# Softmax minus one-hot on one core: 512 columns of the sixth row load on ACT's queue, and ACT's first six rows are written out ahead of its loop

## The chip, the cores and the metric

The kernel runs on one core of one Trainium2 chip. The metric is the device time of one execution in microseconds (us), the median over several runs; smaller is better. The core has five engines with instruction streams of their own: PE (TensorE), DVE (VectorE), ACT (ScalarE), POOL (GpSimd) and SP (SyncE). Transfers between the chip's memory and the core's on-chip memory run on 16 DMA engines. SP and ACT each have a queue on which they issue such transfers.

## The reference

The kernel computes the gradient of the cross entropy: for each of 8 x 1024 rows of 8192 logits, the softmax, less 1 at the row's label.

```
logits_max = np.max(logits, axis=-1, keepdims=True)
exp_logits = np.exp(logits - logits_max)
softmax = exp_logits / np.sum(exp_logits, axis=-1, keepdims=True)
...
one_hot[batch_idx, seq_idx, labels] = 1.0
return (softmax - one_hot).astype(np.float32)
```

Input and output are fp32, 268.4 MB each. Each number is read once and written once.

## The kernel before

**Tiling.** The 8192 rows of the problem are cut into 64 tiles of 128 rows, one row for each of the 128 partitions. The code counts these tiles with t, and the text calls one of them "a row": 128 x 8192 fp32, 4 MB, 32 KB in each partition. Two neighbouring tiles (j = 0 and 1) interleave in memory. The on-chip buffer X holds six rows: SLOTS = 3 times G = 2, so R = 6, and row t lives in slot k = t % 6.

**Steps of a row.** All are done in place in the slot:

1. load (lines 114 to 119): SP issues it on its queue. From row 6 on it waits until the store of the slot's previous row has landed (semaphore `put`). Row 5 waits for `w_iota` instead: an iota of 8192 int16 numbers is first made in the first half of slot 5 and copied from there into PSUM by DVE.
2. `row_max` (line 121): DVE, negated maximum over the row, waits for the load (semaphore `got`).
3. `row_exp` (line 127): ACT, exponential with the maximum as bias, with the row sum accumulated.
4. `invert` (line 133): DVE, reciprocal of the sum.
5. `row_scale` (line 139): ACT, multiplies the row by it.
6. `subtract` (line 145): DVE, subtracts 1 where the iota equals the label.
7. `store` (line 152): ACT issues it on its own queue, after waiting for the subtraction (semaphore `sub`).

**Order.** It is written out by hand; semaphores connect the engines. SP issues all 64 loads in the order of the rows, one behind the other. DVE and ACT each do row 0's maximum and exponential ahead, and then run a hardware loop of ROUNDS = 10 rounds with six rows in each, sixty rows in all. In DVE's loop (lines 172 to 180) row k's turn is: `invert` of row k, `row_max` of row k + 1, `subtract` of row k. In ACT's loop (lines 183 to 192) it is: `row_scale` of row k, `row_exp` of row k + 1, `store` of row k. The counts that the semaphores have to reach are held in registers (`done`, `landed`) that each round raises. The last four rows stand behind the loops; the very last one is scaled and subtracted in four quarters and stored in two halves.

Every operation goes through the helper `run` (line 56), which gives all waits but the last to the engine as instructions of their own and the last one to the operation. That is why nearly every row of the profile carries line 67.

Of the kernel before, what the change touches and what calls it, by code (L numbers as in the profile page):

```python
# [8 lines left out]
G = 2  # L9
SLOTS = 3  # L10
R = SLOTS * G


LAST = 4


@with_exitstack
def kernel(
# [6 lines left out]
    nc = tc.nc  # L25
# [8 lines left out]
    N, V = x_nv.shape  # L34
# [3 lines left out]
    x_b = x_nv.rearrange("(b p j) v -> b p j v", p=P, j=G)  # L38
    o_b = o_nv.rearrange("(b p j) v -> b p j v", p=P, j=G)
# [16 lines left out]
    with tc.tile_critical():  # L56
        sem = tc.alloc_semaphore
        got = [[sem(f"got{i}{q}") for q in range(2)] for i in range(SLOTS)]
        put = [[sem(f"put{i}{q}") for q in range(2)] for i in range(SLOTS)]
        lab_got, dve, pe, pool = (sem(n) for n in ("lab_got", "dve", "pe", "pool"))  # L60
        count = {}

        def run(engine, waits, counter, method, **operands):

            for w in waits[:-1]:
                engine.wait_ge(*w)
            instruction = getattr(engine, method)(**operands)  # L67
            for w in waits[-1:]:
                instruction._wait_ge(*w)
            step = 16 if method == "dma_start" else 1  # L70
            instruction.then_inc(counter, step)
            count[counter.name] = count.get(counter.name, 0) + step
            return counter, count[counter.name]
# [6 lines left out]
            out=ident[:], in_=ident[:], compare_op=Alu.not_equal, fill=1.0,  # L80
# [10 lines left out]
        for j in range(G):  # L91
            w = run(
                nc.tensor, [w_ident, w_lab], pe, "transpose",
                out=lab_ps[:, j, :], in_=lab_f[:, j, :], identity=ident[:],
# [4 lines left out]
            out=iota[:].bitcast(i32), in0=made.bitcast(i32), scalar1=0, scalar2=None, op0=Alu.bitwise_or,  # L99
# [6 lines left out]
        max_of, exp_of, inv_of, scl_of, sub_of = map(per_parity, ("max", "exp", "inv", "scl", "sub"))  # L106

        def slot(k):
            return X[:, k // G, k % G, :]

        def column(a, k):
            return a[:, k : k + 1]

        def load(t):
            b, j = divmod(t, G)
            k = t % R
            after = [(put[k // G][q], t // R * 16) for q in range(G)] if t >= R else []
            after = after[j : j + 1] or [w_iota] * (t == R - 1)
            run(nc.sync, after, got[k // G][j], "dma_start", out=slot(k), in_=x_b[b, :, j, :])

        def row_max(k, n):
            run(
                nc.vector, [(got[k // G][k % G], n)], max_of[k % G], "tensor_reduce",
                out=column(m, k), in_=slot(k), axis=mybir.AxisListType.X, op=Alu.max, negate=True,
            )

        def row_exp(k, n):
            run(
                nc.scalar, [(max_of[k % G], n)], exp_of[k % G], "activation", out=slot(k),
                in_=slot(k), func=Act.Exp, bias=column(m, k), scale=1.0, accum_out=column(s, k),  # L130
            )
# [7 lines left out]
        def row_scale(k, n, c=slice(0, V)):  # L139
            run(  # L140
                nc.scalar, [(inv_of[k % G], n)], scl_of[k % G], "activation", out=slot(k)[:, c],
                in_=slot(k)[:, c], func=Act.Copy, bias=0.0, scale=column(r, k),
            )
# [8 lines left out]
        def store(k, n, target, c=slice(0, V)):  # L152
            run(
                nc.scalar, [(sub_of[k % G], n)], put[k // G][k % G], "dma_start",
                out=target[:, c], in_=slot(k)[:, c],
            )

        def counter(engine, first):
            reg = engine.alloc_register(f"from{first}")
            engine.reg_mov(reg, first)  # L160
            return reg

        ROUNDS = T // R
        for t in range(T):
            load(t)

        row_max(0, 16)
        row_exp(0, 1)

        done = [counter(nc.vector, q + 1) for q in range(SLOTS)]  # L170
        landed = counter(nc.vector, 16)
        with nc.vector.Fori(0, ROUNDS * SLOTS, SLOTS) as b:  # L172
            for k in range(R):
                invert(k, done[k // G])
                if k == R - 1:
                    nc.vector.reg_add(landed, landed, 16)
                row_max((k + 1) % R, landed)
                subtract(k, done[k // G], lab[:, k % G, bass.ds(b + k // G, 1)])
            for reg in done:
                nc.vector.reg_add(reg, reg, SLOTS)  # L180

        done = [counter(nc.scalar, q + 1) for q in range(SLOTS)]
        with nc.scalar.Fori(0, ROUNDS * SLOTS, SLOTS) as b:
            for k in range(R):
                row_scale(k, done[k // G])
                if k == R - 1:
                    for reg in done[: SLOTS - 1]:
                        nc.scalar.reg_add(reg, reg, SLOTS)
                row_exp((k + 1) % R, done[(k + 1) % R // G])
                target = o_b[bass.ds(b + k // G, 1), :, k % G, :]  # L190
                store(k, done[k // G], target.rearrange("o p v -> (o p) v"))
            nc.scalar.reg_add(done[-1], done[-1], SLOTS)

        for t in range(ROUNDS * R, T - 1):
            k, n = t % R, t // G + 1
            invert(k, n)
            row_max(k + 1, 16 * (ROUNDS + 1))
            row_scale(k, n)
            row_exp(k + 1, n + k % G)
            subtract(k, n, lab[:, t % G, t // G : t // G + 1])  # L200
            store(k, n, o_b[t // G, :, t % G, :])
        k, n = (T - 1) % R, B
        invert(k, n)
        for q in range(4):
            c = slice(q * V // 4, (q + 1) * V // 4)
# [41 lines left out]
```

## Time and profile before

| what | value |
|---|---|
| median of three runs | 1247.6 us (1247.5 to 1247.87) |
| span of the profiled execution | 1245.6 us |
| DVE busy in it | 1121.8 us (90%) |
| ACT busy in it | 919.4 us (74%) |
| bytes moved | 268.50 MB read, 268.44 MB written |

The span counts from the first to the last instruction of one profiled execution. It is 2.0 us below the median of the runs, and the steps of that execution are compared with its own span.

How to read the rows: a row of the timeline has the start in us, the duration, the engine, the line, the operation, and its output and input as "out<-in" with partitions x elements; the square brackets give idle time of the engine ahead of it, and what ended that. A "q" behind an engine's name (ACTq, SPq, DVEq) means its sequencer, which issues transfers, does register work and waits. A row of stretches has the stretch, its length, then for PE, its weight loads, DVE, ACT and POOL the busy time with a count of instructions, then PE's clock, the DMA engines' share of busy time and GB/s. A row of a DMA queue has packets, MB and the share of 16 engines' time; q1 is SP's queue, q10 ACT's. A packet is counted where it ends, so in short stretches the share can be over 100%.

### The profile page before, as it was taken

How to read it: one execution, taken by the hardware profiler on the slowest of the kernel's cores; microseconds unless marked ns; L12 is line 12 of the kernel's file. 1: busy time of each engine (PE TensorE's matmuls, PEld its weight loads, DVE VectorE, ACT ScalarE, POOL GpSimd, SP SyncE). 2: the span in 40 equal slices, each digit the busy share in tenths (PEclk: the TensorE clock that was granted, in tenths of full speed). 3: DMA queues.
4: the chain of work that ended last, by engine and by line, in shares of the span. 5: the costliest groups of instructions: out<-in, count | busy, mean ns of one | idle time of the engine just before them, and what ended most of it. 6: DMA issues, size and time to landing. Idle time of an engine off the chain costs nothing.

```text
span 1245.6 us, 868 instructions
## 1 busy us (share of the span) xinstructions
PE 0.4 (0%) x2; PEld 0.3 (0%) x2; DVE 1121.8 (90%) x198; ACT 919.4 (74%) x196; POOL 7.4 (1%) x7
## 2 busy tenths in 40 slices
PE   0000000000000000000000000000000000000000
PEld 0000000000000000000000000000000000000000
DVE  5999999999988989889898898988988989889893
ACT  3888888888767777777767777677777777777772
POOL 2000000000000000000000000000000000000000
DMA  9999999999999999999999999999999999999999
GB/s 406 418 426 436 438 434 425 438 438 429 429 438 436 427 434 438 435 426 436 438 432 426 438 438 428 430 438 435 428 434 438 434 427 436 437 434 426 438 436 389
DMA packets 18625, 536.95 MB, mean 431 GB/s; under 512 B 2080, under 2 KB 2080, under 8 KB 2112
## 3 DMA queue, kind: packets, MB, share of 16 engines
q1 hardware_dynamic: 9216, 268.44, 50.0%
q10 hardware_dynamic: 9408, 268.51, 49.9%
q14 instruction: 1, 0.01, 0.0%
HBM read 268.50 MB, written 268.44 MB: 431 GB/s over the span
## 4 chain that ended last, share of the span: by engine, by line
another core or an unknown queue 67%; DVE 21%; DMA 6%; issue 2%; SPq 1%; DVEq 0%; ACT 0%; ACTq 0%; PE 0%
DVE m L67 11%; DVE X L67 10%; DMA out_dram<-X 4%; DMA X<-in_logits_dram 2%; SPq L67 1%; DVE iota L67 0%; DVE lab_f L67 0%; DMA lab_raw<-in_labels_dram 0%; DVEq L56 0%; ACT X L67 0%; DVE r L67 0%; PE iota L67 0%; ACTq L67 0%; DVEq L172 0%
## 5 line engine op out<-in xcount | busy, mean ns | idle before, releaser
L67 DVE TENSOR_REDUCE m<-X 128x1 f32<-128x8192 f32 x64 | 555.6, 8681 | 90.6 <-DMA X<-in_logits_dram 90.6
L67 ACT ACTIVATE X<-X,m 128x8192 f32<-128x8192 f32 x64 | 455.8, 7122 | 184.8 <-DVE m L67 184.8
L67 DVE SCALAR_TENSOR_TENSOR X<-iota,lab,X 128x8192 f32<-128x8192 int16 (+1 forms) x67 | 559.8, 8360 | 2.4 <-ACT X L67 2.4
L67 ACT ACTIVATE X<-X,r 128x8192 f32<-128x8192 f32 (+1 forms) x67 | 456.4, 6816 | 118.2 <-DVE r L67 118.2
L67 DVE RECIPROCAL r<-s 128x1 f32<-128x1 f32 x64 | 9.8, 153 | 7.3 <-ACT X L67 7.3
L67 ACT ACTIVATION_READ_ACCUMULATOR X<-X,m 128x1 f32 x64 | 11.9, 186 | 0.0
L67 DVE CAST lab_f<-lab_raw 32x256 f32<-32x256 int32 x1 | 3.8, 3784 | 4.6 <-DMA lab_raw<-in_labels_dram 4.6
L67 POOL IOTA X<- 128x8192 int16 x1 | 6.9, 6943 | 0.0
L67 DVE TENSOR_SCALAR iota<-X 128x4096 int32<-128x4096 int32 x1 | 4.4, 4428 | 0.1
L67 ACT ACT_TABLE_LOAD x1 | 1.3, 1283 | 1.4 <-SPq L56 1.4
L67 DVE COPY lab<-iota 128x64 f32<-128x64 f32 x1 | 0.2, 225 | 0.5 <-PE iota L67 0.5
L67 PE MATMUL iota<-ident,lab_f 32*128 32x32 f32 x2 | 0.4, 298 | 8.5 <-DVE lab_f L67 8.5
L67 PEld LDWEIGHTS iota<-ident,lab_f 32*128 32x128 f32 x2 | 0.3, 192 | 8.4 <-DVE lab_f L67 8.4
L67 POOL TENSOR_SCALAR_AFFINE_SELECT ident<-ident 32x32 f32<-32x32 f32 x1 | 0.2, 202 | 0.1
L67 POOL MEMSET ident<- 32x32 f32 x1 | 0.1, 114 | 0.5 <-SPq L56 0.5
L231 POOL MEMSET const-bfloat16-1.0<- 128x1 bf16 x1 | 0.1, 107 | 0.0
L231 POOL MEMSET const-uint8-127<- 128x1 uint8 x1 | 0.1, 107 | 0.0
L231 POOL MEMSET const-float32-0.0<- 128x1 f32 x1 | 0.1, 104 | 0.2 <-issue 0.2
L231 POOL MEMSET const-float32-1.0<- 128x1 f32 x1 | 0.1, 104 | 0.0
## 6 DMA issues: line engine op xcount, KB each, us to landing
X<-in_logits_dram SPq DMA_DIRECT2D x64, 4096.0 KB, 24.2
out_dram<-X ACTq DMA_DIRECT2D x63, 4096.0 KB, 55.2
out_dram<-X ACTq DMA_DIRECT2D x2, 2048.0 KB, 16.9
lab_raw<-in_labels_dram ACTq DMA_DIRECT2D x1, 64.0 KB, 3.7
```

The source lines that it names most:

```text
L67: instruction = getattr(engine, method)(**operands)
L231: nc = _bacc.Bacc("TRN2", target_bir_lowering=False, num_devices=1)
```

## The change

Three things change.

The load of row 5 is split. SP loads the first 7680 of its 8192 columns, at the same place in its queue and behind the same wait. The other 512 columns (`SLAB`; 128 pieces of 2 KB, 256 KB in all) are loaded by a new function `load_rest`, issued on ACT's queue with a semaphore of its own, `rest_got`, and no wait.

`row_max` of slot 5 waits for `rest_got` to reach 16 ahead of its wait for `got`. The instruction stands in DVE's loop, so it is met in each of the ten rounds, though `rest_got` is raised only once.

ACT's first six rows are written out ahead of its loop, with constants as semaphore counts and addresses; `load_rest` stands among them, after the exponential of row 1 and ahead of the store of row 0. The loop runs over the remaining nine rounds, and its counters begin at SLOTS + 1 and up. DVE's loop keeps its ten rounds. A constant `LAST`, which nothing used, is gone.

```
-LAST = 4
+SLAB = 512
...
-        lab_got, dve, pe, pool = (sem(n) for n in ("lab_got", "dve", "pe", "pool"))
+        lab_got, dve, pe, pool, rest_got = (sem(n) for n in ("lab_got", "dve", "pe", "pool", "rest_got"))
...
-            run(nc.sync, after, got[k // G][j], "dma_start", out=slot(k), in_=x_b[b, :, j, :])
+            c = slice(0, V - SLAB) if t == R - 1 else slice(0, V)
+            run(nc.sync, after, got[k // G][j], "dma_start", out=slot(k)[:, c], in_=x_b[b, :, j, c])
+
+        def load_rest():
+            c = slice(V - SLAB, V)
+            run(
+                nc.scalar, [], rest_got, "dma_start",
+                out=slot(R - 1)[:, c], in_=x_b[SLOTS - 1, :, G - 1, c],
+            )
 
         def row_max(k, n):
+            rest = [(rest_got, 16)] if k == R - 1 else []
             run(
-                nc.vector, [(got[k // G][k % G], n)], max_of[k % G], "tensor_reduce",
+                nc.vector, rest + [(got[k // G][k % G], n)], max_of[k % G], "tensor_reduce",
                 out=column(m, k), in_=slot(k), axis=mybir.AxisListType.X, op=Alu.max, negate=True,
             )
...
-        done = [counter(nc.scalar, q + 1) for q in range(SLOTS)]
-        with nc.scalar.Fori(0, ROUNDS * SLOTS, SLOTS) as b:
+        for t in range(R):
+            k, n = t % R, t // G + 1
+            row_scale(k, n)
+            row_exp((k + 1) % R, (t + 1) // G + 1)
+            if t == 0:
+                load_rest()
+            store(k, n, o_b[t // G, :, t % G, :])
+
+        done = [counter(nc.scalar, SLOTS + q + 1) for q in range(SLOTS)]
+        with nc.scalar.Fori(SLOTS, ROUNDS * SLOTS, SLOTS) as b:
             for k in range(R):
                 row_scale(k, done[k // G])
                 if k == R - 1:
```

## The prediction

> **What bounds the kernel now.** I read the page first: span, DMA row, bytes, chain.
>
> ```profile
> span 1245.6 us, 868 instructions
> ...
> PE 0.4 (0%) x2; PEld 0.3 (0%) x2; DVE 1121.8 (90%) x198; ACT 919.4 (74%) x196; POOL 7.4 (1%) x7
> ...
> DMA  9999999999999999999999999999999999999999
> ...
> HBM read 268.50 MB, written 268.44 MB: 431 GB/s over the span
> ...
> another core or an unknown queue 67%; DVE 21%; DMA 6%; issue 2%; SPq 1%; DVEq 0%; ACT 0%; ACTq 0%; PE 0%
> ```
>
> The DMA engines are busy in all forty slices; no compute engine is. The chain's largest share carries no name, so the chain in order of time comes next, with the longest wait of SP's own queue:
>
> ```profile
> 254.75 8.58 DVE m L67
> ...
> 272.02 49.67 DMA out_dram<-X
> 321.71 0.33 SPq L67
> 322.04 18.97 another core or an unknown queue
> 341.02 0.33 SPq L67
> ...
> 1174.07 24.22 DMA X<-in_logits_dram
> 1198.31 8.69 DVE m L67
> ```
> ```profile
> SPq L67 <- DMA out_dram<-X: 1140.4, 58, 57.2
> ```
>
> From 322 us on the piece without a name lies between one load's issue and the next, and SP's queue says what it waits for: a store that has to land, 58 times. Up to 272 the chain runs through DVE. That could suggest that the early part is bound by DVE, so I asked for the rate by stretch (the last two numbers are DMA share and GB/s):
>
> ```profile
> 3.00:47.00 44.00, 0.41 (x2) 0.28 (x2) 34.49 (x9) 21.55 (x5) 5.25 (x1) 1.00 1.00 429
> 47.00:71.00 24.00, 0.00 (x0) 0.00 (x0) 24.00 (x5) 20.66 (x4) 0.00 (x0) 1.00 1.00 415
> 71.00:272.00 201.00, 0.00 (x0) 0.00 (x0) 201.00 (x37) 165.71 (x36) 0.00 (x0) 1.00 1.00 433
> 322.00:1174.00 852.00, 0.00 (x0) 0.00 (x0) 765.87 (x133) 630.46 (x133) 0.00 (x0) 1.00 1.00 433
> 1198.00:1233.00 35.00, 0.00 (x0) 0.00 (x0) 26.54 (x7) 20.74 (x7) 0.00 (x0) 1.00 1.01 435
> ```
>
> The engines are as full where DVE leads the chain (433 GB/s) as where the loads wait for stores (433). So the whole time is bytes over rate. DVE is only the first to be asked in a stretch where six preloaded slots give it work. A change counts if it changes the bytes, what a packet costs, or leaves both DMA queues empty at once.
>
> How the queues share the engines: in steady work, the 20 us from 342, and in three successive microseconds from 57 to 60:
>
> ```profile
> q10 hardware_dynamic: 144, 4.19, 48.6%
> q1 hardware_dynamic: 144, 4.19, 48.6%
> ```
> ```profile
> q1 hardware_dynamic: 16, 0.52, 121.3%
> q10 hardware_dynamic: 16, 0.52, 121.3%
> q1 hardware_dynamic: 16, 0.52, 121.3%
> ```
>
> q1 is SP's queue (loads), q10 ACT's (stores). A row is 144 packets: 128 of 32 KB and 16 tiny ones, so 8 + 1 for each engine. The queues take turns packet by packet: sixteen of one, then sixteen of the other. 121.3% of 16 engines for 1 us over 16 packets is 1.21 us a packet, and 16 x 1.21 = 19.4 us is the distance between loads in the chain (322.04 to 341.02 with the issue, 19.3).
>
> **The change part by part.** The span ends with the stores' last bytes, so I sum against 1245.6.
>
> *Bytes.* The slab, 128 rows of 2 KB, leaves SP's sixth load and goes to ACT's queue: none saved, none added. An engine's eight packets of row 5 shrink from 32 to 30 KB: by the rate 8 x 1.21 / 16 = 0.61 us less. It gets eight packets of 2 KB more. Before has such packets, the labels' 32, in the first 5 us:
>
> ```profile
> q10 hardware_dynamic: 48, 0.07, 5.0%
> ...
> lab_raw<-in_labels_dram ACTq DMA_DIRECT2D x1, 64.0 KB, 3.7
> ```
>
> 5.0% of 16 x 5 us is 4.0 us of engine time over 32 packets (the 16 tiny ones are next to nothing): 0.125 us each. Eight are 1.00 us. Net +0.4 us. From below: packets at the bulk rate, 0.076 us each, net 0. From above: the slab holds every engine as long as the label load took from issue to landing, 3.7 - 0.6 = +3.1. I take +0.4, since the label packets are of the same size.
>
> *When the slab starts, and what stands behind it.* It has no wait of its own, but stands behind the second exponential on ACT:
>
> ```profile
> 38.32 7.12 ACT L67 ACTIVATE X<-X,m 128x8192 f32<-128x8192 f32 x1 [1.46 <-DVE m L67]
> 46.97 0.39 ACTq L67 DMA_DIRECT2D out_dram<-X  x1
> ...
> 98.86 8.67 DVE L67 TENSOR_REDUCE m<-X 128x1 f32<-128x8192 f32 x1
> ...
> 116.17 8.67 DVE L67 TENSOR_REDUCE m<-X 128x1 f32<-128x8192 f32 x1
> ```
> ```profile
> L67 ACTq MOVE out_dram<-X x60: 29/29/35, 38.4 to 1149.0; - x60
> ```
>
> ACT's sequencer computed the first store's address at 38.4, while the exponential had only begun; so the slab issues near 38.4 and costs the sequencer about the 0.39 us of a store's issue, in time in which it waits for DVE until 46.97. SP's queue is full then, so eight small packets take turns with eight of 32 KB: 8 x (1.21 + 0.13) = 10.7 us, after a start of 2.5 (worked out below), landing near 52. Row 5's maximum starts at 98.86, so DVE's new wait finds the slab landed with some 46 us in hand; all that DVE does is queued behind that wait, which is why this margin matters. The first store is asked for at 46.97 and can wait behind the slab's last packets for about 2 us (47 + 2.5 against 52). Late next is then the load of row 6, which SP issues when that store has landed (71.22), and behind it in SP's queue every later load:
>
> ```profile
> 71.22 18.47 SPq L67 DMA_DIRECT2D X<-in_logits_dram  x2
> ```
>
> It lands some 24 us later, near 95, for a maximum at 116.17: 20 us in hand. SP moves exactly the bytes that ACT's queue did not, so the engines stay full. Cost 0.
>
> *First bytes.* There is a dip where the first store joins:
>
> ```profile
> 48.00:52.00 4.00, 0.00 (x0) 0.00 (x0) 4.00 (x1) 4.00 (x1) 0.00 (x0) 1.00 0.89 279
> 52.00:56.00 4.00, 0.00 (x0) 0.00 (x0) 4.00 (x2) 2.90 (x2) 0.00 (x0) 1.00 1.03 442
> ```
>
> (433 - 279) x 4 us is 0.62 MB, or 1.4 us; a window cuts packets of 0.52 MB, so this is rough (1.0 us by the row from 47 to 71). With the slab, ACT's queue joins earlier and lightly: between -1.4 (the dip goes) and +1.4 (it comes twice). I take 0, as the store joins all the same.
>
> *Fixed start of a DMA.* The first two loads:
>
> ```profile
> DMA to landing us min/median/max: 12.2/16.9/21.5
> ```
>
> 12.2 us for eight packets of 1.21 leaves 2.5 us of start and finish. The second, queued behind it, took 21.5, only 9.3 more, so that latency overlaps and takes no engine time. The Trainium skill ("DMA: Bandwidth & Descriptors", section "Anatomy of one DMA") gives each DMA a fixed cost of about 2.0 us, which speaks against splitting one. If all of it fell on the engines, the sum would be 2.0 us above before, an estimate from that page; the row shows it as latency under other work, and I don't add it.
>
> *ACT's loop, DVE's wait.* Six rows written out drop six rounds of address arithmetic on ACT; DVE gets a second wait before row 5's maximum, once in each of ten rounds, about as dear as its existing register step:
>
> ```profile
> L67 DVEq FUSED_REGOPS  x60: 53/57/71, 29.6 to 1140.2; - x60
> ...
> DVE m L67 <- DMA X<-in_logits_dram: 90.6, 47, 2.0
> ```
>
> At 0.07 us, two or three fall in DVE's stretch before 272 (0.2 us, hidden by the queued stores), the others in the up to 2.0 us that DVE then waits for each load. Without that cover, 0.7 us in all. Cost 0.
>
> *The end.* Would a delay of the computation reach it? The last row's two half stores are issued from 1222.74; packets of SP and ACT in 1226 to 1232, then 1232 to 1238:
>
> ```profile
> q10 hardware_dynamic: 80, 2.62, 101.1%
> ```
> ```profile
> q10 hardware_dynamic: 155, 2.54, 98.7%
> ```
>
> 80 packets of 32 KB are still whole rows; only then come the 16 KB packets of the half rows. So the last row stands in the queue for some 10 us, less 2.5 of start: 7 us of delay are free.
>
> Sum: 1245.6 + 0.4 = 1246.0. The runs' median, 1247.6, is 2.0 above the span, so **1248.0**; its own range, with the dip's -1.4 and the slab's +3.1, is 1246.2 to 1250.7.
>
> **The rivals.**
>
> *A. The slab doesn't go early.* ACT could issue it only after the exponential, at 45.5. Its eight turns would last until 57 and the first store would stand behind them, 6 us late; load 6 too, against 20 us in hand. The loads meanwhile have the engines alone (429 in the row of 3 to 47). Again 1248.0. For it: the slab stands behind that instruction. Against: the address step at 38.4. By the Trainium skill (same page, "Queues, rings and completion order") an engine drains a packet of 9 to 17 descriptors before it switches queues; the slab, nine for each engine, would then be through in a microsecond and A could not happen. The rows from 57 to 60 show turns of one 32 KB piece, so the trace does not agree.
>
> *B. Slower: the engines lose step.* A row's semaphore is complete when the slowest of 16 engines is. If unequal packets (2 and 30 KB) leave engines apart, each hand-over from store to load comes late, and the 415 GB/s of 47 to 71 hold on to 272, where the chain leaves DVE: 201 x (433/415 - 1) = 8.7 us, so 1248.0 + 8.7 = 1256.7. It decides from the point at which the rate after 71 drops below 433 by 1.2%. For it: 279 GB/s where the queues met. Against: 442 right after.
>
> *C. Faster: a better pitch.* Loads alone, from 3.8 to 48 us:
>
> ```profile
> DMA packets 670, 19.33 MB, mean 437 GB/s; under 512 B 80, under 2 KB 80, under 8 KB 80
> ```
>
> If the shift of one sixteenth of a row let the mixture run at 437 from 71 to 1198: 1127 x (1 - 433/437) = 10.3 us less, 1237.7. For it: some rate is left. Against: turns are by packet whatever the shift, and stores alone reach 435 at most.
>
> **How the numbers follow.** 0.2%, or 2.5 us, is about what a measurement of this kernel tells from no change: 1245.1 to 1250.1. Forecast 0.66, A 0.12, B 0.14, C 0.08. Forecast and A end within the bound: same 0.78, slower 0.14, faster 0.08. The 80% range reaches a little to both sides, for partial B or C: 1244.5 to 1251.5.
>
> **What would show it.** Right: a load of 256 KB issued near 38.4 and landing near 52; DVE's maximum of row 5 at about 98.9 without idle time; 19.4 us from load to load; 433 GB/s in the long stretch; half-row packets only from about 1233. Wrong: idle DVE before row 5's maximum; the first store issued later than 47; under 428 GB/s between 71 and 272 (B); over 435 in the long stretch (C); any slice of the DMA row below 9.

## The result: slower by 0.3%, and scattered

| kernel | median | lowest to highest | executions |
|---|---|---|---|
| before | 1247.77 us | 1247.40 to 1248.17 | 21 |
| changed | 1250.35 us | 1247.91 to 1264.19 | 21 |

The ratio of the means is 1.0032, with an interval of 1.0020 to 1.0044: 4.0 us. At the median the change costs 2.6 us; the mean is higher because the slow executions lie far out. The scatter says more: before, 21 executions lie within 0.8 us; changed, the fastest lies within the range of before (1247.91), and the others reach up to 16 us more. Something in the changed kernel comes out differently each time. (Ratios leave out an execution over 1.5% above the fastest of its kernel; below that concerns only one, of 1275.8 us, in experiment 5.)

The profiled execution of the changed kernel took 1255.35 us, 5 above its median; experiment 11 has a second one, of 1250.59. The page of the first:

```profile
span 1253.2 us, 863 instructions
...
DMA  9999999999999999999999999999999999999997
...
HBM read 268.50 MB, written 268.44 MB: 428 GB/s over the span
...
X<-in_logits_dram SPq DMA_DIRECT2D x63, 4096.0 KB, 28.5
out_dram<-X ACTq DMA_DIRECT2D x63, 4096.0 KB, 50.9
...
X<-in_logits_dram ACTq DMA_DIRECT2D x1, 256.0 KB, 15.7
```

The bytes are the same; the span is 7.6 us longer. The last number of an issue row is the median time to landing: loads take 28.5 us where they took 24.2 (experiment 9 shows that this alone costs nothing). The last of the forty slices of the DMA row is at 7; of the prediction's signs of being wrong, it is the one that came. Next, the rate by stretch (DMA share and GB/s at the end of each row), first the main stretches, then the tail:

```profile
47.00:71.00 24.00, 0.00 (x0) 0.00 (x0) 24.00 (x5) 20.66 (x4) 0.00 (x0) 1.00 1.01 422
71.00:272.00 201.00, 0.00 (x0) 0.00 (x0) 199.75 (x35) 165.71 (x36) 0.00 (x0) 1.00 1.00 431
322.00:1174.00 852.00, 0.00 (x0) 0.00 (x0) 765.46 (x133) 629.57 (x132) 0.00 (x0) 1.00 1.00 433
```
```profile
1224.00:1226.00 2.00, 0.00 (x0) 0.00 (x0) 1.68 (x2) 0.20 (x2) 0.00 (x0) 1.00 0.34 147
1226.00:1246.00 20.00, 0.00 (x0) 0.00 (x0) 9.13 (x4) 7.68 (x4) 0.00 (x0) 1.00 0.99 423
1246.00:1251.50 5.50, 0.00 (x0) 0.00 (x0) 0.00 (x0) 0.00 (x0) 0.00 (x0) 1.00 0.20 83
```

The tail of the kernel before, for comparison:

```profile
1224.00:1226.00 2.00, 0.00 (x0) 0.00 (x0) 2.00 (x2) 0.00 (x0) 0.00 (x0) 1.00 0.84 360
1226.00:1243.50 17.50, 0.00 (x0) 0.00 (x0) 1.23 (x1) 0.00 (x0) 0.00 (x0) 1.00 0.98 419
```

The long stretch runs at 433 GB/s as before. The loss lies mostly in the tail: from 1224 to 1226 the engines are two thirds empty, and from 1246 to the end only a fifth of them works. A fifth of 16 engines is three: some engines finish 5 us later than the others. (The 0.84 of before comes from counting a packet where it ends: by the packet records its engines have no idle time there.)

The chain shows why they are empty at 1224:

```profile
1179.79 28.45 DMA X<-in_logits_dram
1208.24 0.02 issue
1208.27 8.69 DVE m L67
1216.95 8.67 DVE X L67
1225.62 0.02 issue
1225.64 0.34 ACTq L67
```

The last load lands at 1208.24, 10 us later than before (1198.29). The store of row 62 is therefore issued at 1225.64 rather than 1215.68; the engines that are ahead have by then written all that was queued.

**How far the engines are apart.** Each row's transfer ends with 16 tiny packets, one for each engine, written when that engine has done its share. From the trace's packet records I took the time from the first to the last of each sixteen, the spread. In us, row by row for the first rows of the store queue:

```
row             0    1    2    3    4    5  ...  18   40
before         0.5  0.5  0.5  0.5  0.5  0.5 ... 0.5  0.6
changed        2.2  4.7  4.4  4.4  4.4  4.4 ... 11.3 11.3
```

Before, the sixteen engines stay within 0.6 us of one another through the stretch, and within 0.9 at the very end. Changed, they are 2.2 us apart after the first store, 4.7 after the second, and 11.3 from row 17 to row 58; the last rows have 8.3 and then 4.9 to 5.4. The two queues' rows for three successive microseconds, 80 to 83, of the changed kernel show it directly; where before has 16 packets of one queue and then 16 of the other, each queue has some:

```profile
q10 hardware_dynamic: 7, 0.23, 53.1%
q1 hardware_dynamic: 4, 0.13, 30.3%
...
q1 hardware_dynamic: 9, 0.29, 68.3%
q10 hardware_dynamic: 7, 0.23, 53.1%
...
q10 hardware_dynamic: 8, 0.26, 60.6%
q1 hardware_dynamic: 5, 0.16, 37.9%
```

**Where the 7.6 us are.** What packets took beyond their usual 1.213 us (1.138 for 30 KB), counted where it is over 0.03, adds up to 48 us of engine time after the first 4 us, against 18 before: 3.0 and 1.1 us for each of 16 engines, so +1.9. The dry spell is 2 us at 0.34, 1.3 lost. The end is 5.5 us at 0.20, 4.4 lost. Sum 7.6. The edges of the last two stretches were chosen by eye, so an agreement to the tenth is luck. A reading without such edges: of the last transfer's sixteen tiny packets the first is through at 1246.07 (1243.04 before), the last 5.43 us later (0.85 before). So 3.0 us are lost by all engines, and 4.6 by the last one.

### The profile page after: what moved, and what is told of

It is laid out like the page before. It is cut to its first block, busy times and chain, and to the rows that moved or that the text cites. A ratio compares the mean times of both kernels' runs of the same rounds, so it can differ in the third digit from the quotient of the medians.

```text
span 1253.2 us, 863 instructions
## 1 busy us (share of the span) xinstructions
PE 0.4 (0%) x2; PEld 0.3 (0%) x2; DVE 1119.3 (89%) x198; ACT 919.3 (73%) x196; POOL 7.4 (1%) x7
## 4 chain that ended last, share of the span: by engine, by line
another core or an unknown queue 70%; DVE 18%; DMA 7%; issue 1%; SPq 1%; ACT 1%; DVEq 0%; PE 0%; ACTq 0%
DVE m L67 9%; DVE X L67 8%; DMA out_dram<-X 4%; DMA X<-in_logits_dram 2%; SPq L67 1%; ACT X L67 1%; DMA lab_raw<-in_labels_dram 1%; DVE iota L67 0%; DVEq L56 0%; DVE r L67 0%; DVE lab_f L67 0%; PE iota L67 0%; ACTq L67 0%; DVE lab L67 0%
## 5 line engine op out<-in xcount | busy, mean ns | idle before, releaser
L67 DVE CAST lab_f<-lab_raw 32x256 f32<-32x256 int32 x1 | 1.0, 1036 | 7.4 <-DMA lab_raw<-in_labels_dram 7.4
## 6 DMA issues: line engine op xcount, KB each, us to landing
X<-in_logits_dram SPq DMA_DIRECT2D x63, 4096.0 KB, 28.5
```

## The experiments

My theory after the result: the slab's small packets and the first store stand in ACT's queue together; engines that still have slab packets left and engines that have none meet the store at different points of their turns, and from there the sixteen are out of step. Each kernel below differs from the changed kernel by the edit shown. Each ratio is against executions of the kernel before that were taken along with it, 24 to 33 of them. Three of these 89 took longer than the others (1249.25, 1250.09 and 1251.44 us, the others under 1248.5), so the kernel before is not quite free of scatter. "Spread" is the median spread of the store queue's rows between 600 and 1150 us in the kernel's profiled execution.

### 1. Only the rows written out

```
-            c = slice(0, V - SLAB) if t == R - 1 else slice(0, V)
+            c = slice(0, V)
...
-            rest = [(rest_got, 16)] if k == R - 1 else []
+            rest = []
...
-            if t == 0:
-                load_rest()
```

> ACT's first six rows are written out, and row 5 loads whole on SP's queue: the change without the slab. Theory (the slab's small packets, met by the first store on the same queue, put the 16 DMA engines out of step with one another): without the slab they stay in step; median 1247.5 to 1248.2 with all runs within 1 us, load landing 24.2 us after issue. Rival (the written-out rows, with other issue times on ACT, do it): 1249 to 1252 with single runs up to 1260, landing 26 to 29.

Measured: 1247.73 us (1247.48 to 1247.89, 11 executions), ratio 0.9999 (0.9990 to 1.0008), spread 0.7. The landing and the end of the chain are those of before:

```profile
X<-in_logits_dram SPq DMA_DIRECT2D x64, 4096.0 KB, 24.2
```
```profile
1174.10 24.21 DMA X<-in_logits_dram
1198.33 8.69 DVE m L67
```

The rows written out cost nothing. What costs is the slab, or DVE's wait for it, which is gone here too.

### 2. The slab on SP's queue, behind row 5

```
 def load_rest():
...
-                nc.scalar, [], rest_got, "dma_start",
+                nc.sync, [], rest_got, "dma_start",
...
         for t in range(T):
             load(t)
+            if t == R - 1:
+                load_rest()
```

The call among ACT's rows is gone.

> As the changed kernel, but the slab is issued on SP's queue right behind the rest of row 5: the same packets of 30 and 2 KB and the same second wait on DVE, and no load on ACT's queue. Theory (slab and first store share ACT's queue): in step, 1247.5 to 1248.5, scatter under 1 us. Rival 1 (unequal packet sizes are enough, wherever they are queued): 1249 to 1252 with scatter of several us. Rival 2 (DVE's second wait): 1249 to 1252 with the landing unchanged at 24.2.

Measured: 1249.05 us (1247.86 to 1253.37, 11), ratio 1.0013 (1.0004 to 1.0022), spread 1.5. That is a miss for the theory as I put it: without any load on ACT's queue there is half of the loss at the median and some of the scatter, just inside what rival 1 foretold. Small packets among stores can loosen the engines from SP's queue as well. Rival 2, DVE's second wait, went with an unchanged landing of 24.2; it changed:

```profile
X<-in_logits_dram SPq DMA_DIRECT2D x63, 4096.0 KB, 33.3
```

The landing turns out to be a poor sign (experiment 9). What speaks against the second wait is that experiments 3, 7 and 8 have it too and do not scatter.

### 3. The slab behind the first row's exponential

```
         row_exp(0, 1)
+        load_rest()
...
-            if t == 0:
-                load_rest()
```

> As the changed kernel, but the slab stands behind the first row's exponential, so it is issued near 22 us and is through near 36, some 10 us ahead of the first store. Theory (slab and first store meet while some engines have slab packets left and others none): the meeting is gone, so in step, 1247.5 to 1248.5, scatter under 1 us. Rival (small packets that take turns with loads put the engines out of step by themselves): 1249 to 1252, scatter of several us.

Measured: 1248.46 us (1247.85 to 1248.85, 11), ratio 1.0005 (0.9996 to 1.0014), spread 1.3. The issues on ACT's queue:

```profile
22.30 0.36 ACTq L67 DMA_DIRECT2D X<-in_logits_dram  x1
46.97 0.35 ACTq L67 DMA_DIRECT2D out_dram<-X  x1
```

The slab lands 14.8 us after 22.30, 10 us before the first store is issued. The same slab, with the same turns between small and large packets, leaves the engines nearly in step.

### 4. The slab behind the first store

```
+            store(k, n, o_b[t // G, :, t % G, :])
             if t == 0:
                 load_rest()
-            store(k, n, o_b[t // G, :, t % G, :])
```

> As the changed kernel, but the slab is issued on ACT's queue behind the store of row 0 rather than ahead of it. The first store meets the loads as in the kernel before. Theory (the first store must meet the loads with all engines at the same point): the first meeting is clean, but the slab's packets then lie between two stores; if only the first meeting counts, 1247.5 to 1248.5 with small scatter. Rival (small packets on ACT's queue do it, wherever they stand): 1249 to 1252, scatter of several us.

Measured: 1248.70 us (1248.53 to 1249.04, 11), ratio 1.0008 (0.9999 to 1.0017), spread 1.2. No scatter to speak of; the median is 0.2 over the theory's bound. Small packets between two stores do little harm; ahead of the first store they do.

### 5. A slab of 128 columns

```
-SLAB = 512
+SLAB = 128
```

> The changed kernel with a slab of 128 columns: the same number of small packets at the same place, a quarter of their bytes. Theory (what counts is that eight small packets of each engine take turns with loads and still stand in ACT's queue when the first store arrives, not their bytes): out of step as in the changed kernel, median 1249.5 to 1251.5, the slowest run over 1253. Rival (the bytes by which loads and stores are shifted): between before and the changed kernel, 1247.8 to 1248.8, scatter under 1.5 us.

Measured: 1250.85 us (1248.01 to 1275.8, 11), ratio 1.0025 (1.0008 to 1.0042). A quarter of the bytes, the same loss: the bytes are not what counts. Its profiled execution was the slowest of all; it is shown as an extreme, and no conclusion rests on it alone. Spread 18.2 us, and a tail with two dry spells:

```profile
1225.00:1230.00 5.00, 0.00 (x0) 0.00 (x0) 5.00 (x1) 3.83 (x2) 0.00 (x0) 1.00 0.15 66
1230.00:1240.00 10.00, 0.00 (x0) 0.00 (x0) 7.97 (x3) 7.12 (x1) 0.00 (x0) 1.00 0.98 419
1240.00:1250.00 10.00, 0.00 (x0) 0.00 (x0) 9.75 (x3) 7.21 (x2) 0.00 (x0) 1.00 0.11 46
1250.00:1270.00 20.00, 0.00 (x0) 0.00 (x0) 9.13 (x4) 7.68 (x4) 0.00 (x0) 1.00 0.98 420
```

From 503 us on its chain no longer runs through one queue; it goes round through load, DVE and store:

```profile
1151.31 44.43 DMA out_dram<-X
1195.76 36.55 DMA X<-in_logits_dram
1232.34 8.69 DVE m L67
```

With engines 18 us apart, a load is complete only after 36.55 us, and the last one lands 34 us later than in the kernel before.

### 6. The first store waits for the slab

```
             if t == 0:
                 load_rest()
+                nc.scalar.wait_ge(rest_got, 16)
```

> The changed kernel, with ACT waiting for the slab to land (near 54 us) before it goes on to the first store. The slab stays where it is, the first store is 7 us later and alone in its queue. Theory (slab and first store must not be in the queue together): in step, median 1248.2 to 1248.9, scatter under 1.5 us, load landing near 24.2. Rival (the slab taking turns at this place is enough): 1249.5 to 1251.5, slowest over 1253. If the 7 us themselves reach the end, 1255, without scatter.

Measured: 1248.88 us (1248.43 to 1249.65, 11), ratio 1.0009 (1.0000 to 1.0018), spread 2.8.

```profile
38.32 0.36 ACTq L67 DMA_DIRECT2D X<-in_logits_dram  x1
53.36 0.35 ACTq L67 DMA_DIRECT2D out_dram<-X  x1
```

The slab is issued in the same instant as in the changed kernel, the first store 6.4 us later, and the scatter shrinks from 16 us to 1.2. This kernel delays ACT's next scaling by 6.4 us (53.76 for 47.37) and DVE's next subtraction by 5.4 (60.91 for 55.51), and is still faster at the median than the changed one: most of that vanishes under the transfers, as the prediction's reading of the early part has it. Against before it costs 1.2 us, with a spread of 2.8.

### 7. The slab one instruction earlier

```
+            if t == 0:
+                load_rest()
             row_exp((k + 1) % R, (t + 1) // G + 1)
-            if t == 0:
-                load_rest()
```

> The changed kernel with the slab issued one instruction earlier on ACT, behind the scaling of row 0 near 29.8 us rather than behind the exponential of row 1 near 38.3: through near 43, before the first store is issued at 47. Theory: in step, 1248.2 to 1248.9, scatter under 1.5 us, as with the slab behind the first exponential. Rival (any slab after the first few loads): 1249.5 to 1251.5 with slowest run over 1253.

Measured: 1248.54 us (1247.83 to 1248.99, 11), ratio 1.0006 (0.9997 to 1.0015), spread 0.9. The issue is at 29.74:

```profile
29.74 0.36 ACTq L67 DMA_DIRECT2D X<-in_logits_dram  x1
46.97 0.35 ACTq L67 DMA_DIRECT2D out_dram<-X  x1
```

Landing 14.6 us later, at 44.3, it is through under 3 us before the first store is issued. That is enough.

### 8. The slab on SP's queue, behind row 0

```
         for t in range(T):
+            if t == 1:
+                load_rest()
             load(t)
```

`load_rest` issues on SP's queue as in experiment 2.

> The slab on SP's queue behind row 0's load rather than behind row 5's: its packets run while no store is under way. Theory (small packets harm only where they meet the other queue's packets): in step, 1247.9 to 1248.6, scatter under 1.5 us, against 1247.9 to 1253.4 with the slab behind row 5, whose packets fall among stores. Rival (row 5's 30 KB packets, which run among stores in both, are what loosens the engines there): scatter up to 1251 or more again.

Measured: 1248.54 us (1247.85 to 1248.87, 11), ratio 1.0004 (0.9995 to 1.0013), spread 1.2. Nearly in step. Row 5's 30 KB packets run among stores here as in experiment 2, so they aren't the cause of the scatter; the place of the 2 KB packets is.

### 9. The first store in two pieces, no slab

```
+            if t == R:
+                after = [(rest_got, 16)] + after
...
             if t == 0:
-                load_rest()
-            store(k, n, o_b[t // G, :, t % G, :])
+                c = slice(V - SLAB, V)
+                run(
+                    nc.scalar, [(sub_of[0], 1)], rest_got, "dma_start",
+                    out=o_b[0, :, 0, c], in_=slot(0)[:, c],
+                )
+                store(k, n, o_b[0, :, 0, :], slice(0, V - SLAB))
+            else:
+                store(k, n, o_b[t // G, :, t % G, :])
```

Row 5 loads whole and DVE has no second wait, as in experiment 1.

> No slab: row 5 loads whole on SP's queue. Instead the first store is issued in two: 512 columns first, in packets of 2 KB, then the other 7680, and the load of row 6 waits for both. So eight small packets of each engine lead ACT's queue at the meeting with the loads, but every engine begins on them at the same point. Theory (what loosens the engines is that some have small packets left when the first store arrives and others have not): in step, 1247.9 to 1248.9, scatter under 1.5 us. Rival (small packets at the meeting, however the engines stand): 1249.5 to 1251.5, slowest over 1253.

Measured: 1247.80 us (1247.50 to 1248.19, 11), ratio 1.0000 (0.9991 to 1.0009), spread 0.7; 0.1 us under the theory's range. Eight small packets on each engine stand right ahead of the first big store packet and cost nothing. They take turns with loads for some 9 us here too (50.5 to 59.7 by the packet records); the difference is that the rest of the store is queued behind them on every engine before they are through. One more thing is seen here:

```profile
X<-in_logits_dram SPq DMA_DIRECT2D x64, 4096.0 KB, 28.5
```

The loads land as late as in the changed kernel, and the time is that of before. So a late landing as such is harmless. Nor does a spread of the loads cost anything here: 2.5 us on SP's queue in the same stretch (0.6 before), while the stores have 0.7. The spread of the stores is the measure.

### 10. A slab of 2048 columns

```
-SLAB = 512
+SLAB = 2048
```

> The changed kernel with a slab of 2048 columns, 8 KB packets: eight turns of about 1.5 us, so the slab ends near 53 us and stands ahead of the first store on nearly all engines. Theory: out of step as with 128 and 512 columns, 1249.5 to 1252, slowest over 1253. Rival (only tiny packets do it): 1247.8 to 1248.8, scatter under 1.5 us.

Measured: 1249.30 us (1247.91 to 1263.85, 11), ratio 1.0023 (1.0000 to 1.0047), spread 5.0. The median is 0.2 under the theory's bound, the scatter that of the changed kernel. 64 KB, 256 KB and 1 MB at this place all scatter; at 1 MB the interval only just reaches no change.

### 11. The changed kernel once more

> The changed kernel once more, for a second trace of it. Theory: its time goes with how far the engines are apart. If this execution is under 1248.8, the loads land 24 to 26 us after issue and the last load before 1201; if it is over 1250, they land 28 or later and the last load lands after 1205. Rival (the spread of the engines is not what costs): a slow execution with landing 24.2, or a fast one with 28.

Measured: five executions, 1251.95 us (1250.59 to 1253.74), ratio 1.0037 (1.0024 to 1.0050); the profiled one 1250.59. Spread 4.6.

```profile
1175.57 27.35 DMA X<-in_logits_dram
1202.94 8.69 DVE m L67
```

The direction is as expected, the bounds are missed (last load landed at 1202.9 rather than after 1205; median landing 27.9). By experiment 9 the landing was the wrong thing to bet on.

### All together

One line for each profiled execution, by spread:

```
kernel                       spread us   time us
before                          0.6       (median 1247.8)
1  rows written out only        0.7      1247.60
9  first store in two           0.7      1247.91
7  slab at 29.7                 0.9      1248.46
8  slab on SP behind row 0      1.2      1248.68
4  slab behind first store      1.2      1248.70
3  slab at 22.3                 1.3      1248.85
2  slab on SP behind row 5      1.5      1248.97
6  store waits for slab         2.8      1249.65
11 changed, once more           4.6      1250.59
10 slab of 2048                 5.0      1251.69
   changed                     11.3      1255.35
5  slab of 128                 18.2      1275.80
```

The time rises with the spread without an exception. It does so only for the stores: by the spread of the loads, experiment 9 with 2.5 would stand behind 2 and 6 (2.2 and 1.7).

**Where the time is lost.** From the packet records, the sixteen tiny packets of the very last transfer: the end of the first, and how much later the last of them ends. All in us.

```
kernel                      first    last later by   span
before                     1243.04       0.85       1245.64
1  rows written out only   1243.05       0.88       1245.70
9  first store in two      1242.66       1.48       1245.92
7  slab at 29.7            1243.04       1.44       1246.27
8  slab on SP behind row 0 1243.00       1.70       1246.48
4  slab behind first store 1243.03       1.70       1246.51
3  slab at 22.3            1243.02       1.85       1246.66
2  slab on SP behind row 5 1243.47       1.53       1246.78
6  store waits for slab    1243.57       2.11       1247.46
11 changed, once more      1242.83       3.79       1248.39
10 slab of 2048            1242.85       5.00       1249.49
   changed                 1246.07       5.43       1253.16
5  slab of 128             1270.14       1.82       1273.61
```

In all but the last two rows the first engine is through within 0.6 us of where it is in the kernel before, and most of what is added to the span is the time by which the last engine comes later. This also bears on whether DVE's second wait costs the quiet kernels their 0.8 us: it should hold back the first engine as well, and in experiments 3, 7 and 8 that one isn't late. Only in the last two rows do all engines lose much time too: in longer packets and in dry spells.

**How the engines part.** On one engine a packet begins when the one before it ends, so the records can be strung into sixteen chains. Each engine has eight packets of the slab.

Row 3's load ends on the sixteen engines between 41.74 and 42.09 us, and in the same 0.4 us the slab arrives. On ten engines its first packet comes ahead of a tiny packet that ends row 3; SP's turn is over with that, and a second slab packet follows at once. On the other six a whole load packet comes first, and the slab begins at 42.95 or later. So ten engines are through with the slab by 50.1 us, ahead of the first store's packets, and six still have their eighth slab packet, which begins at 52.9 to 53.4.

The ten begin the store at 52.6 to 53.2 and row 5's load at 55.0 to 55.6, with two store packets behind them. The six begin row 5's load at 53.1 to 53.5, with no store packet behind them, and the store at 54.2 to 54.6. From here the turns of the two groups differ.

In experiment 11 three engines are late and not six. In experiments 3 and 7 none has slab packets left when the store begins, and in experiment 6, where nine are late with the slab, the store waits for them. That the number of late engines is what makes the executions scatter is inferred from these few traces. It doesn't give the size: experiment 5's execution has five late engines and a larger spread.

## Why the prediction was wrong

- **That the engines are the bound, and full.** Right for the stretch that it was read from: 433 GB/s from 322 to 1174 in both kernels.
- **The sum and its range.** The sum adds up. The range doesn't use all of its own terms: with the dip's +1.4 beside the slab's +3.1 its top would be 1252.1, not 1250.7.
- **When the slab starts.** Right: issued at 38.32, foretold near 38.4, so rival A is out. It landed at 54.0, foretold near 52: its first packet began 3.4 us after the issue, and six engines had to wait for their eighth packet. In the microsecond from 48 the two queues of the changed kernel show 16 loads and 16 small packets:

```profile
q1 hardware_dynamic: 16, 0.52, 121.8%
q10 hardware_dynamic: 16, 0.03, 8.5%
```

- **The delays behind it.** Right in size, partly by luck: before, the first store's packets began 5.2 us after its issue, and the prediction had 2.5 for that as for the slab, so both came 2 to 3 us later than it says. The first store was issued on time, and its first packets began at 52.6 to 54.6 us on the sixteen engines (52.2 to 52.7 before): up to 2 us late, as foretold. Row 6's load was issued 1.7 us later, row 5's maximum not at all:

```profile
46.97 0.35 ACTq L67 DMA_DIRECT2D out_dram<-X  x1
...
72.88 37.64 SPq L67 DMA_DIRECT2D X<-in_logits_dram  x3
...
98.86 8.66 DVE L67 TENSOR_REDUCE m<-X 128x1 f32<-128x8192 f32 x1
```

- **"SP moves exactly the bytes that ACT's queue did not, so the engines stay full. Cost 0." This is the step that failed.** It took the sixteen engines for one pipe, and so put the overlap of the slab with the first store at nothing. The delay of up to 2 us is not one delay: it is 0.4 us on some engines and 2 on others. Nothing pulled them together again in this execution. By the packet records, row 6's load began within 0.5 us on all engines before, and between 76.3 and 79.5 us changed. The sum had 0.4 us for the whole change; it cost 2.6 at the median, 4.0 in the mean and 7.6 in the profiled execution. Experiments 3, 6 and 7 remove that meeting and keep the slab: 1248.5 to 1248.9, scatter 1.0 to 1.2 us.
- **First bytes, 0.** About right: the stretch from 47 to 71 runs at 422 GB/s, 415 before, which is 0.4 us gained, inside the range of 1.4 to both sides.
- **Fixed start.** The 2.0 us that the prediction quotes from the Trainium skill ("DMA: Bandwidth & Descriptors", section "Anatomy of one DMA") are given there for transfers that GpSimd issues; those here are issued by SP and ACT. Nothing in the sum hangs on it: the engines of experiments 3, 7 and 8 are not held up, as the end of the first of them shows.
- **ACT's rows, 0, and DVE's wait, 0.** Experiment 1 confirms the first; the ends of the first engine in experiments 3, 7 and 8 speak for the second.
- **The packets' price, +0.4 us.** Small, and mis-sized: the three quietest slabs (experiments 3, 7, 8) cost 0.8 us at the median, though each one's interval includes no change. The slab's 2 KB packets took 0.084 us where the label packets gave 0.125, so packet time alone is +0.07; the remainder is the last engine's lateness at the end, 1.4 to 1.9 us in place of 0.85. Why even a quiet slab leaves that spread was not settled.
- **The end: 7 us of delay are free.** The reading holds, and was used up: the last load came 10 us later, and the engines ran dry at 1224. Experiment 11's came 4.6 us later, inside the 7, and its engines did not run dry. It was still 2.8 us slower than before, as its last engine ended late. So the reading asked only for a delay of the computation and did not think of one that comes from the transfers themselves.
- **Rival B, the engines lose step.** Its mechanism is what happened, at the place it named, and it had 0.14. Its price was wrong in size and place: it looked for 8.7 us between 71 and 272, where the rate fell only from 433 to 431. Most of the loss is in the tail, where the last of sixteen engines sets the end: 4.6 of 7.6 us in the first profile, all of it in experiment 11's.
- **Rival C**, a better pitch: nothing of it. The long stretch stayed at 433.
- The range held the median: its upper side was there for a part of B, and that is what came, at another place. The forecast of "same" did not hold: its bound was 2.5 us, and the cost is 2.6 at the median and 4.0 in the mean.

What stays open: why the kernel before took longer in 3 of 89 executions, of which there is no trace; and why an uneven start heals in one kernel (experiment 4: 1.8 us apart at the first store, 0.7 some rows later) and grows in another (2.2 to 11.3). The packets that take longer in the changed kernel come in groups of one to ten at the end of a row until about 410 us, which suggests that the hand-over between rows is where it grows; no run isolates that. Experiment 6 keeps a spread of 2.8 though the slab and the store don't meet.

No version here beats the kernel before. Experiments 1 and 9 equal it.

## What to carry to other kernels

A transfer is complete when the slowest of its engines is, so sixteen engines are one pipe only while they are in step; before a small transfer is put beside large ones, ask whether it is through, on every engine, when the next large transfer joins. The same 256 KB cost 0.8 us when they were through 3 us before the first store was issued; without that room they cost 2.6 us at the median, and up to 16 in single executions. And where executions of a kernel scatter though its work does not vary, compare how far the engines of one transfer end apart, before looking at rates.

## What the runs showed of the hardware

- Two queues take turns by single packets: 16 loads of 32 KB and 16 slab packets of 2 KB in the same microsecond, the one from 48 us. The Trainium skill ("DMA: Bandwidth & Descriptors", section "Queues, rings and completion order") has an engine typically drain 9 to 17 descriptors before it switches; the trace does not agree.
- In every kernel looked at packet by packet (before, changed, and experiments 2 to 5), load packets in flight at about 48 to 52 us, when the first store joins, take up to 1.2 us longer than the usual 1.213 us; before, all sixteen take 2.0 to 2.2 us. Why was not looked into.
- In the long stretch of the changed kernel's first profile, engines that have lost step don't find it again: they are 11.3 us apart from row 17 to row 58.
